# A two-layer hybrid trunk in fp32: the odd layer off GpSimd, norm squares summed by TensorE, the recurrence in halves, GELU as one function

## The chip, the cores and the metric

The kernel runs on one core of a Trainium2 chip. The metric is device time in microseconds of the whole program. One core has five engines that the text names as the profile does: PE (TensorE, matrix products into PSUM banks), DVE (VectorE), ACT (ScalarE), POOL (GpSimd) and SP (which issues DMAs).

## The reference

Two layers over a sequence of 512 positions with 1024 features, batch 1, all in fp32. Every sub-layer stands between two RMS norms, and its result is added to the residual:

```
for layer in range(2):
    hn  = rms_norm(x, norm_mix_pre[layer])
    mix = even_mixer(hn, ...) if layer == 0 else odd_mixer(hn, ...)
    x   = x + rms_norm(mix, norm_mix_post[layer])
    hn  = rms_norm(x, norm_ffn_pre[layer])
    ff  = (silu(hn @ w_gate) * (hn @ w_up)) @ w_down          # 2816 hidden
    x   = x + rms_norm(ff, norm_ffn_post[layer])
```

The even mixer is dilated attention beside an S5 state-space layer. The odd mixer, which the change touches most, is a gated recurrence:

```
z  = hn @ w_in                                   # 1024 + 1024 columns
xc = conv4(z[:, :1024]) + conv_b                 # causal, per feature
r, i = sigmoid(xc @ w_r + b_r), sigmoid(xc @ w_i + b_i)   # 4 blocks of 256
a  = exp(-8 * r * softplus(-lam))
h  = scan: h_t = a_t * h_{t-1} + sqrt(1 - a_t^2) * i_t * xc_t
mix = (h * gelu(z[:, 1024:])) @ w_out            # gelu in its tanh form
```

## The kernel before

Features lie on the 128 partitions and positions along the free dimension: the residual is eight tiles `xT[f]` of 128x512. For fp32 precision each operand of a product is split into a high and a low part in a rounded 32-bit type, and a product is three TensorE products (`mm3`: high by high, high by low, low by high). Weights are loaded raw by SP's queue (`Raw`), split by ACT (`whi`, L240) and an engine that the caller names (`wlo`, L241; VectorE unless `eng` says otherwise).

A program scheduler orders each engine's instructions by a simulated timeline. The code ties it down in three ways: `seq_of` and `pe.pin` keep an instruction behind the one traced before it on its engine, `tc.issue_after(ins)` queues what a block traces behind `ins`, and small generators (`start`, `tick`, `drain`) interleave the norm's steps with products by a counted clock.

The stages around the change, in order of time:

- **`out_proj`** (three times: `mo0` at the end of the even mixer, `fd0` after the first FFN, `mo1` after the odd mixer). It forms eight tiles of the result, four at a time. The last `ntail` contraction steps of the second four are done in two halves of 256 positions, and the post-norm of a half (`norm_half`) runs under products: column sums on TensorE, a power on GpSimd (`rstd_of`, L381), a broadcast by TensorE, and then for each feature tile a VectorE product (L492), the residual add (GpSimd, L498, but for the first), a ScalarE copy `xh` (L499) and a VectorE difference `xl` (L487). `half_cols` then multiplies these with the first four column groups of the next stage, half by half. PSUM has six `main` banks, handed out in turn, and two `side` banks.
- **`pre_rstd`** (three times: `f0`, `m1`, `f1`): the pre-norm of the next stage. ACT squares the eight `xT` tiles, VectorE adds four of them (L425), GpSimd the other four (L425), TensorE sums over partitions (`cs`), and `rstd_of` and `bcast_sb` make the row `rb`. In the FFN this is called by `mid()` after the products of the first pair of the main loop; until then the first four column groups wait as plain copies (L614, L616).
- **`ffn_up`**: 20 pairs of gate and up columns by a seven-product scheme (`f00b` to `f03b` and `f10b` to `f13b` are its banks; each pair is 84 TensorE products of 256 columns). Its weights need VectorE sums (L629 to L632) besides the splits, and its first pair needs input combinations (`tr`, `th`, `tl`, L641 on). "Head" below is this stage's first three pairs.
- **`odd_body`**: eight columns `xb`, each evacuated by `conv` (VectorE and ACT); `gates(blk)` for four blocks (sigmoids on ACT, `xc*gi` on GpSimd, L1542); `recurrence()` over all eight tiles at once (exp and tanh on ACT, the square of `a` on GpSimd, L1556, then sqrt, product, scan); `gate_product(f)` for the eight gate columns; `gate_out` (GELU from its parts: a GpSimd square L1576, VectorE, ACT's tanh, VectorE); `gated` (product with the scan, split into `y1h`, `y1l` for the output projection).

Of the kernel before, what the change touches and what calls it, by code (L numbers as in the profile page):

```python
# [11 lines left out]
F32 = mybir.dt.float32  # L12
# [3 lines left out]
ALU = mybir.AluOpType  # L16
# [3 lines left out]
P = 128  # L20
# [74 lines left out]
def hybrid_trunk(  # L95
# [318 lines left out]
    def pre_rstd(nm, keep=None):  # L414
        accs = []
        for f in (0, 4, 1, 5, 2, 6, 3, 7):
            eng = dve if f < NF // 2 else pool
            if f % (NF // 2) == 0:
                accs.append(sb.tile([P, S], F32, tag="sqacc", bufs=2, name=f"sqacc_{nm}{f}"))
                act.activation(accs[-1], xT[f], AF.Square)  # L420
            else:
                q = sb.tile([P, S], F32, tag="sq", bufs=2, name=f"sq_{nm}{f}")
                act.activation(q, xT[f], AF.Square)
                acc = accs[f // (NF // 2)]
                eng.tensor_tensor(acc, acc, q, op=ALU.add)  # L425
        return rstd_of(col_sums(lambda t: [a[:, t * P:(t + 1) * P] for a in accs], 0, NT, nm, "mid"), NT, nm,
                       keep=keep)

    def out_proj(wget, ks, yh, yl, pname, layer, nm, otile, gname, glayer, ntail, tail_alloc, early, eng0=None,
# [15 lines left out]
        for i in range(4):  # L445
# [26 lines left out]
        ready.clear()  # L472

        def norm_half(h):
# [15 lines left out]
            for f in range(NF):  # L490
# [8 lines left out]
                seq_of(act.activation(xh[f][:, HS[h]], xf, AF.Copy, scale=col(gname, glayer * NF + f)))  # L499
# [28 lines left out]
        return xh, xl, (first, bs)  # L528
# [56 lines left out]
    def ffn_up(layer, xh, xl, first, nm, hp):  # L585
# [11 lines left out]
        def mid():  # L597
            env["rb"] = bcast_sb(pre_rstd(nm, eps), nm, "mid")
# [80 lines left out]
        for n in range(NFIRST // 2, NH):  # L679
# [61 lines left out]
    def ffn(layer, xh, xl, first):  # L741
# [922 lines left out]
```

## Time and profile before

| | us |
|---|---|
| median of 3 runs (lowest to highest) | 1211.34 (1208.27 to 1212.36) |
| the profiled execution | 1211.84 |
| its span, first to last instruction | 1210.1 |

The page of the profile gives busy time by engine, the span in 40 slices of 30.25 us, the chain that ended last, and groups of instructions by line. A window's row holds, for a stretch of the span, its length, then for each engine its busy time and number of instructions, then the granted TensorE clock (1.00 is full), the DMA share and GB/s. In a waits row `A <- B: t, n, m`, A waited for B t us in all, n times, at most m. In a timeline row the numbers are start and duration; in brackets stands the idle time before it and what ended it. A line that says `x4` is four instructions merged. Matmul records are those of single passes: one fp32 product by `ones` or `ident` leaves two.

### The profile page before, as it was taken

To read this page: it belongs to the slowest core of one execution; us is meant where nothing else is said; L and a number is where in the kernel's file an instruction comes from. 1 tells how busy PE (TensorE), PEld (TensorE's weight loads), DVE (VectorE), ACT (ScalarE), POOL (GpSimd) and SP (SyncE) were. 2 spreads that over 40 slices of the span, in tenths; PEclk is the share of its full clock that TensorE was granted. 3 is DMA by queue.
4 is the path that set the end of the run, shared out by engine and by line. 5 is a ranking of instruction groups with operands and counts; after the bars stand their busy time and mean duration, and the time that the engine had idled before them with its cause. 6 is when DMAs were issued, how large, how long until landed. Compare 5 with 4: busy or idle time off the path is not lost.

```text
span 1210.1 us, 19987 instructions
## 1 busy us (share of the span) xinstructions
PE 1138.7 (94%) x7406; PEld 1012.8 (84%) x7406; DVE 905.5 (75%) x1823; ACT 622.9 (51%) x1255; POOL 181.9 (15%) x173
## 2 busy tenths in 40 slices
PE   7899999999699999999999999599799999999997
PEld 6787766888699999988889878389689999988886
DVE  7978775369789998983327897977989998894224
ACT  6555576448455545652334467354755455482222
POOL 2000020432400000000135045434310000000001
PEclk9899899999799999999999999799999999999999
DMA  8344410712233323332331223140243233343321
GB/s 207 103 137 128 110 47 1 192 36 70 70 96 105 89 79 105 107 108 94 120 96 36 87 88 105 53 135 6 69 122 97 84 100 89 105 131 105 97 69 70
DMA packets 165273, 113.44 MB, mean 94 GB/s; under 512 B 26820, under 2 KB 141752, under 8 KB 165176
## 3 DMA queue, kind: packets, MB, share of 16 engines
q1 hardware_dynamic: 161848, 109.94, 30.9%
q10 hardware_dynamic: 3040, 2.17, 0.7%
q8 instruction: 58, 0.95, 0.3%
q14 instruction: 39, 0.32, 0.1%
q0 software_dynamic: 288, 0.07, 0.0%
HBM read 103.75 MB, written 4.19 MB: 89 GB/s over the span
## 4 chain that ended last, share of the span: by engine, by line
PE 57%; DVE 6%; issue 5%; ACT 3%; DMA 3%; POOL 2%; SPq 0%; DVEq 0%; POOLq 0%; ACTq 0%
PE op_fd L170 10%; PE fo L170 10%; PE f00b L170 4%; PE f01b L170 4%; PE f02b L170 4%; PE f12b L170 4%; PE f10b L170 4%; PE f11b L170 4%; PE op_mo L170 2%; PE f03b L170 2%; PE f13b L170 2%; PE fd0b L170 2%; POOL sqacc_f L425 2%; PE xbb L170 2%; PE mo1b L170 1%
## 5 line engine op out<-in xcount | busy, mean ns | idle before, releaser
L241 DVE TENSOR_TENSOR wlo_fo<-wraw_fo,whi_fo 128x512 fp32r<-128x512 f32 x44 | 30.3, 691 | 64.0 <-PE fo L170 58.1
L170 PE MATMUL op_fd<-hi_f,whi_fd 128*128 128x512 f32 (+1 forms) x200 | 73.5, 368 | 0.0
L170 PE MATMUL op_fd<-lo_f,whi_fd 128*128 128x512 f32 (+1 forms) x200 | 73.2, 366 | 0.0
L170 PE MATMUL op_fd<-hi_f,wlo_fd 128*128 128x512 f32 (+1 forms) x200 | 72.9, 368 | 0.0
L241 DVE TENSOR_TENSOR wlo_fd<-wraw_fd,whi_fd 128x512 fp32r<-128x512 f32 x44 | 30.6, 705 | 55.2 <-ACT whi_fd L240 41.1
L170 PE MATMUL fo<-wlo_fo,hi_f 128*128 128x512 f32 x176 | 69.6, 396 | 0.0
L170 PE MATMUL fo<-whi_fo,lo_f 128*128 128x512 f32 x176 | 69.2, 394 | 0.0
L170 PE MATMUL fo<-whi_fo,hi_f 128*128 128x512 f32 x176 | 68.8, 395 | 0.0
L240 ACT ACTIVATE whi_fo<-wraw_fo 128x512 fp32r<-128x512 f32 x44 | 27.3, 631 | 71.4 <-DMA wraw_fo<-in_ffn_w_down_dram 45.1
L240 ACT ACTIVATE whi_fd<-wraw_fd 128x512 fp32r<-128x512 f32 x44 | 27.3, 630 | 56.4 <-DMA wraw_fd<-in_ffn_w_down_dram 36.4
L811 POOL TENSOR_SCALAR s<-ss,eps_f 128x1 f32<-128x1 f32 x4 | 1.1, 266 | 298.6 <-ACT fsq L809 298.6
L170 PE MATMUL op_mo<-y1l,whi_mo 128*128 128x256 f32 (+1 forms) x88 | 31.6, 361 | 13.2 <-DVE y1l L1587 13.2
L170 PE MATMUL qkv<-whi_qkv,xh_m 128*128 128x512 f32 x96 | 42.4, 443 | 1.3 <-DVE up L1196 1.0
L170 PEld LDWEIGHTS op_fd<-lo_f,whi_fd 128*128 128x128 f32 x200 | 37.7, 189 | 6.8
L170 PEld LDWEIGHTS op_fd<-hi_f,wlo_fd 128*128 128x128 f32 x200 | 37.7, 188 | 6.6
L170 PEld LDWEIGHTS op_fd<-hi_f,whi_fd 128*128 128x128 f32 x200 | 37.7, 188 | 6.4
L170 PE MATMUL qkv<-wlo_qkv,xh_m 128*128 128x512 f32 x96 | 39.3, 410 | 2.8 <-DVE wlo_qkv L241 2.8
L241 POOL TENSOR_TENSOR wlo_mo<-wraw_mo,whi_mo 128x512 fp32r<-128x512 f32 x22 | 34.0, 1576 | 50.1 <-ACT whi_mo L240 50.1
L453 POOL TENSOR_TENSOR oacc_fd<-oacc_fd,osq_fd 128x512 f32<-128x512 f32 x3 | 4.2, 1409 | 247.7 <-ACT osq_fd L452 247.6
L629 DVE TENSOR_TENSOR wraw_s_f<-wraw_f,wraw_f 128x512 f32<-128x512 f32 x40 | 27.5, 688 | 18.3 <-DMA wraw_f<-in_ffn_w_up_dram 14.1
L170 PEld LDWEIGHTS fo<-whi_fo,lo_f 128*128 128x128 f32 x176 | 33.1, 188 | 7.8
L170 PEld LDWEIGHTS fo<-whi_fo,hi_f 128*128 128x128 f32 x176 | 33.1, 188 | 7.8
(1987 smaller groups left out, 4482.7 us busy)
## 6 DMA issues: line engine op xcount, KB each, us to landing
wraw_f<-in_ffn_w_gate_dram SPq DMA_DIRECT2D x88, 256.0 KB, 3.2
wraw_f<-in_ffn_w_up_dram SPq DMA_DIRECT2D x88, 256.0 KB, 3.2
wraw_fd<-in_ffn_w_down_dram SPq DMA_DIRECT2D x44, 256.0 KB, 2.6
wraw_fo<-in_ffn_w_down_dram SPq DMA_DIRECT2D x44, 256.0 KB, 2.9
wraw_qkv<-in_ev_w_in_dram SPq DMA_DIRECT2D x24, 256.0 KB, 3.4
wraw_mo<-in_ev_w_out_dram SPq DMA_DIRECT2D x16, 256.0 KB, 4.9
wraw_xb<-in_od_w_in_dram SPq DMA_DIRECT2D x16, 256.0 KB, 3.2
wraw_gg<-in_od_w_in_dram SPq DMA_DIRECT2D x16, 256.0 KB, 3.0
```

The source lines that it names most:

```text
L170: self.pin(nc.tensor.matmul(o, lhsT=lhsT, rhs=rhs, start=start, stop=stop, **kw))
L240: act.activation(hi, src, AF.Copy)
L241: eng.tensor_tensor(lo, src, hi.bitcast(F32), op=ALU.subtract)
L425: eng.tensor_tensor(acc, acc, q, op=ALU.add)
L453: pool.tensor_tensor(acc, acc, q, op=ALU.add)
L629: dve.tensor_tensor(s1, a21, a22, op=ALU.add)
L811: pool.tensor_scalar(s0, ss[:, 0:1], 1.0 / D, eps[:, t:t + 1], op0=ALU.mult, op1=ALU.add)
```

## The change

1. `pre_rstd` goes. `norm_half` squares each half tile of the new residual on ACT right behind `xh`, and `next_sums` sums a pair of tiles over partitions by TensorE products with a column of ones into a bank `nsum` that is taken out of the six `main` banks until the stage ends. `mid()` takes `rstd_of(nsum)`.
2. In the FFN `mid()` moves ahead of the main loop; the first four column groups are evacuated with `rb` and gated at once.
3. The squares' adds in `out_proj` (L453), the `wlo` splits of `mo0`, `mo1` and the first four `xb` columns, and `xc*gi` go from GpSimd to VectorE; the square of `a` goes from GpSimd to ACT.
4. `recurrence` runs over tiles 0 to 3 after blocks 0 and 1, and over 4 to 7 after blocks 2 and 3. The sigmoids of blocks 2 and 3 are queued behind the first half's last sqrt. `gi` lies in the convolution's `xp` buffers.
5. GELU is one ACT function, queued behind the second half's last sqrt.

```diff
-    def pre_rstd(nm, keep=None):
-        ...
@@ out_proj
-                pool.tensor_tensor(acc, acc, q, op=ALU.add)
+                dve.tensor_tensor(acc, acc, q, op=ALU.add)
...
+        nb = sets["main"].pop(0)
+        share(next=(nb,))
+        nsum = bank(f"ns_{nm}", "next")
+        def next_sums(h, fs, q):
+            for i, f in enumerate(fs):
+                for t in range(2):
+                    c = 2 * h + t
+                    pe.pin(nc.tensor.matmul(nsum[:, c:c + 1], lhsT=q[:, i * HT + t * P:i * HT + (t + 1) * P],
+                                            rhs=ones[:, 0:1], start=(c == 0 and f == 0), stop=(f == NF - 1),
+                                            skip_group_check=True))
@@ norm_half, for f in range(NF)
                 seq_of(act.activation(xh[f][:, HS[h]], xf, AF.Copy, scale=col(gname, glayer * NF + f)))
+                if f % 2 == 0:
+                    q = sb.tile([P, S], F32, tag="sqacc" if h else "sq", bufs=2, name=f"nsq_{nm}{h}{f}")
+                seq_of(act.activation(q[:, HS[f % 2]], xf, AF.Square))
                 late.append(f)
+                if f % 2 and f > 1:
+                    next_sums(h, (f - 3, f - 2), qlast)
+                if f % 2:
+                    qlast = q
...
+            next_sums(h, (NF - 2, NF - 1), qlast)
@@ ffn_up
-                dve.tensor_copy(env[n][0], b)
+                dve.tensor_tensor(env[n][0], b, env["rb"], op=ALU.mult)
             else:
                 act.activation(env[n][1], b, AF.Copy)
+                gated(*env[n], n)
         heads = gemm_cols(cols2[:NFIRST], first, xh, xl, nm, evac)
         next(heads)
+        mid()
...
-            if n == NFIRST // 2:
-                mid()
-                for i in range(n):
-                    dve.tensor_tensor(env[i][0], env[i][0], env["rb"], op=ALU.mult)
-                    gated(*env[i], i)
@@ out_proj and first_cols of mo0, mo1, xb: the argument pool goes
@@ odd_body, gates
-                        t = sb.tile([P, S], F32, tag="ut", bufs=2, name=f"gi{f}")
-                    last["sig"] = act.activation(t, b, AF.Sigmoid, bias=col(bn, f)).ins
-                pool.tensor_tensor(xc[f], xc[f], t, op=ALU.mult)
+                        t = lp.tile([P, S + 3], F32, tag="xp", bufs=2, name=f"gi{f}")[:, 0:S]
+                    with ExitStack() as order:
+                        if after is not None:
+                            order.enter_context(tc.issue_after(after))
+                        last["sig"] = act.activation(t, b, AF.Sigmoid, bias=col(bn, f)).ins
+                dve.tensor_tensor(xc[f], xc[f], t, op=ALU.mult)
@@ recurrence(fs): over fs instead of all, and
-                    pool.tensor_tensor(m, al[f], al[f], op=ALU.mult)
+                    act.activation(m, a, AF.Square)
@@ gate_out goes; gate_product(f) ends with g = bank * rb
@@ gated
+            with tc.issue_after(last["sqrt"]):
+                act.activation(g, g, AF.Gelu_apprx_tanh)
             dve.tensor_tensor(g, g, xc[f], op=ALU.mult)
...
@@ the order
         gates(0)
         gates(1)
-        bs = [gate_product(0)]
-        gates(2)
-        bs.append(gate_product(1))
-        gates(3)
-        gg = [gate_out(f, bs[f]) for f in range(2)]
-        recurrence()
+        gg = [gate_product(0)]
+        recurrence(range(NF // 2))
+        gg += [gate_product(1), gate_product(2)]
+        gates(2, last["sqrt"])
+        gates(3, last["sqrt"])
+        gg.append(gate_product(3))
+        recurrence(range(NF // 2, NF))
         for f in range(NF):
-            if f >= 2:
-                bs.append(gate_product(f))
-                gg.append(gate_out(f, bs[f]))
-            if f >= 3:
-                gated(f - 3, gg[f - 3])
-        for f in range(NF - 3, NF):
             gated(f, gg[f])
+            if f + 4 < NF:
+                gg.append(gate_product(f + 4))
```

More of the change, by code (lines that the diff above doesn't have):

```diff
@@ L412, in xg_tiles @@
                 [sb.tile([P, S], F32R, tag="xl", bufs=NF, name=f"xl_{nm}{f}") for f in range(NF)])
-    def pre_rstd(nm, keep=None):
[L415 to L427, printed above, removed]
     def out_proj(wget, ks, yh, yl, pname, layer, nm, otile, gname, glayer, ntail, tail_alloc, early, eng0=None,
@@ L527, in out_proj @@
         in_order[0] = False
-        return xh, xl, (first, bs)
+        sets["main"].insert(0, nb)
+        return xh, xl, (first, bs), nsum
     def rows_of(w):
@@ L583, in ffn_cols, with ffn_up @@
         return [(w[layer], n * P) for n in range(NH) for w in (ffn_w_gate, ffn_w_up)]
-    def ffn_up(layer, xh, xl, first, nm, hp):
+    def ffn_up(layer, xh, xl, first, nsum, nm, hp):
         cols2 = ffn_cols(layer)
@@ L597, in mid @@
         def mid():
-            env["rb"] = bcast_sb(pre_rstd(nm, eps), nm, "mid")
+            env["rb"] = bcast_sb(rstd_of(nsum[:, 0:NT], NT, nm, keep=eps), nm, "mid")
         def gated(gt, ut, n):
@@ L739, in spare, with ffn @@
         return sb.tile([P, S], F32, tag="gt" if i < 2 else "ut", bufs=2, name=name)
-    def ffn(layer, xh, xl, first):
+    def ffn(layer, xh, xl, first, nsum):
         with tc.tile_pool(name=f"hid{layer}", bufs=1) as hp:
@@ L744, in ffn @@
             share(side=(6, 7))
-            hh, hl, eps = ffn_up(layer, xh, xl, first, f"f{layer}", hp)
+            hh, hl, eps = ffn_up(layer, xh, xl, first, nsum, f"f{layer}", hp)
             def otile(i, name):
@@ L757, in ffn, with ffn_last @@
             got = out_proj(rows_of(ffn_w_down[layer]), list(range(NH)), hh, hl, "p1", layer, f"fd{layer}", otile,
-                           "g0", layer + 1, 6, alloc, lambda: first_cols(odd_cols(), "xb", pool), eps=eps)
+                           "g0", layer + 1, 6, alloc, lambda: first_cols(odd_cols(), "xb"), eps=eps)
             places[:] = [p for p in places if p[0] is sb]
         return got
-    def ffn_last(xh, xl, first):
+    def ffn_last(xh, xl, first, nsum):
         hp = ctx.enter_context(tc.tile_pool(name="hid1", bufs=1))
@@ L765, in ffn_last @@
         share(side=(6, 7))
-        hh, hl, eps = ffn_up(1, xh, xl, first, "f1", hp)
+        hh, hl, eps = ffn_up(1, xh, xl, first, nsum, "f1", hp)
         xk = [None] * (2 * NT)
@@ L1522, in odd_body, with gates @@
         last = {}
-        def gates(blk):
+        def gates(blk, after=None):
             raw = Raw(4, 256, f"rg{blk}")
@@ L1550, in recurrence @@
                     last["exp"] = act.activation(gr[f], gr[f], AF.Tanh, scale=sp8[:, f:f + 1]).ins
+                    m = sb.tile([P, S], F32, tag="sq", bufs=2, name=f"lm{f}")
+                    act.activation(m, a, AF.Square)
+                    dve.scalar_tensor_tensor(gr[f], m, 1.0, gr[f], op0=ALU.add, op1=ALU.mult)
                     al.append(a)
             with tc.issue_after(last["exp"]):
-                for f in range(NF):
-                    m = sb.tile([P, S], F32, tag="sq", bufs=2, name=f"lm{f}")
-                    pool.tensor_tensor(m, al[f], al[f], op=ALU.mult)
-                    dve.scalar_tensor_tensor(gr[f], m, 1.0, gr[f], op0=ALU.add, op1=ALU.mult)
+                for f in fs:
                     last["sqrt"] = act.activation(gr[f], gr[f], AF.Sqrt).ins
-            for f in range(NF):
+            for f in fs:
                 dve.tensor_tensor(gr[f], gr[f], xc[f], op=ALU.mult)
@@ L1585, in gated @@
             l = lp.tile([P, S], F32R, tag="cl", bufs=NF, name=f"y1l{f}")
-            act.activation(h, g, AF.Copy, scale=0.5)
-            dve.scalar_tensor_tensor(l, g, 0.5, h.bitcast(F32), op0=ALU.mult, op1=ALU.subtract)
+            act.activation(h, g, AF.Copy)
+            dve.tensor_tensor(l, g, h.bitcast(F32), op=ALU.subtract)
             yh.append(h)
@@ L1628, in hybrid_trunk @@
         return
-    xh, xl, first = odd_layer(xh, xl, first)
+    xh, xl, first, nsum = odd_layer(xh, xl, first, nsum)
     for f in range(NF):
         dump(f"x3_{f}", xT[f])
-    ffn_last(xh, xl, first)
+    ffn_last(xh, xl, first, nsum)
 _INS = ['x', 'positions', 'norm_mix_pre', 'norm_mix_post', 'norm_ffn_pre', 'norm_ffn_post',
```

27 lines of the change are left out of this document (10 added, 17 removed).

## The prediction

> **What bounds the kernel now.** I read the page's busy times and slices first, then the windows, then the waits of the two places where TensorE falls back, then the timelines there.
>
> ```profile
> span 1210.1 us, 19987 instructions
> PE 1138.7 (94%) x7406; PEld 1012.8 (84%) x7406; DVE 905.5 (75%) x1823; ACT 622.9 (51%) x1255; POOL 181.9 (15%) x173
> PE   7899999999699999999999999599799999999997
> POOL 2000020432400000000135045434310000000001
> PEclk9899899999799999999999999799999999999999
> ```
>
> TensorE is the bound: 94% busy. Its dips lie where GpSimd works: slices 11, 26 and 29 (around 300, 770 and 870 us), with the granted clock down in them too. The windows show the lag. Columns: length, then busy time and count of PE, PEld, DVE, ACT, POOL, then the clock.
>
> ```profile
> 360.00:380.00 20.00, 20.00 (x170) 20.00 (x170) 20.00 (x41) 10.81 (x22) 0.00 (x0) 1.00 0.37 107
> 560.00:580.00 20.00, 20.00 (x87) 16.12 (x87) 7.03 (x11) 5.64 (x10) 0.27 (x1) 1.00 0.29 93
> 284.00:346.00 62.00, 48.20 (x330) 46.07 (x330) 50.66 (x100) 37.40 (x73) 13.89 (x5) 0.86 0.31 90
> 852.00:905.00 53.00, 41.67 (x289) 39.04 (x288) 45.34 (x90) 32.63 (x67) 13.41 (x4) 0.90 0.30 86
> 667.00:760.00 93.00, 92.09 (x406) 74.28 (x404) 80.16 (x126) 57.56 (x94) 34.40 (x25) 1.00 0.30 91
> 760.00:807.00 47.00, 32.38 (x115) 24.48 (x114) 45.85 (x55) 21.33 (x36) 17.74 (x12) 0.82 0.29 90
> ```
>
> The first two rows are TensorE undisturbed: 20/170 = 0.118 us for a product of 256 columns, 20/87 = 0.230 us for one of 512. By these prices the 330 products of the first FFN head (284 to 346) need 38.8 us and took 62: 23.2 lost. The second head (852 to 905): 289 need 34.0 of 53: 19.0 lost. Odd output projection (760 to 807): 115 need 26.4 of 47: 20.6 lost. Until 760 the odd layer loses nothing. Together 62.8 us, lost clock included. What ends the waits:
>
> ```profile
> PE f02b L170 <- ACT pv_f L696: 4.6, 1, 4.6
> ACT sq_f L423 <- POOL sqacc_f L425: 7.8, 1, 7.8
> PE f12b L170 <- ACT pv_f L696: 5.6, 1, 5.6
> PE op_mo L170 <- DVE y1l L1587: 13.2, 2, 9.8
> ```
>
> In the heads TensorE waits for a ScalarE copy, and ScalarE stands behind a square whose buffer GpSimd holds. The timeline says why GpSimd holds it so long:
>
> ```profile
> 302.76 9.46 POOL L425 TENSOR_TENSOR sqacc_f<-sqacc_f,sq_f 128x512 f32<-128x512 f32 x1 [18.72 <-issue]
> 303.06 0.68 DVE L629 TENSOR_TENSOR wraw_s_f<-wraw_f,wraw_f 128x512 f32<-128x512 f32 x1
> ...
> 310.42 0.68 DVE L241 TENSOR_TENSOR wlo_f04c<-wraw_s_f,whi_f04c 128x512 fp32r<-128x512 f32 x1
> 660.21 1.30 POOL L425 TENSOR_TENSOR sqacc_m<-sqacc_m,sq_m 128x512 f32<-128x512 f32 x1
> 312.25 0.63 ACT L423 ACTIVATE sq_f<-xT 128x512 f32<-128x512 f32 x1 [7.85 <-POOL sqacc_f L425]
> ```
>
> The same add takes 1.30 us elsewhere. Here it ends 1.1 us after VectorE's unbroken run does: it was shut out for 8.2 us. In the odd layer it goes the other way round:
>
> ```profile
> 712.69 6.63 POOL L1542 TENSOR_TENSOR xc<-xc,gi 128x512 f32<-128x512 f32 x4 [2.05 <-ACT gi L1541]
> 712.38 0.68 DVE L241 TENSOR_TENSOR wlo_rg<-wraw_rg,whi_rg 128x512 fp32r<-128x512 f32 x1
> 712.98 1.78 DVE L1508 SCALAR_TENSOR_TENSOR xc<-xp,cols,xc 128x512 f32<-128x512 f32 x1
> ```
>
> While GpSimd runs, a VectorE instruction of 0.68 takes 1.78 us: 1.10 extra. The last two windows count 25 and 12 GpSimd instructions, by the code 34 of them whole tiles (8 `xc*gi`, 8 squares of `a`, 8 of GELU's, 10 `wlo_mo`). That is up to 37 us lost on an engine that is 45.85 of 47 us busy and that TensorE waits for.
>
> The Trainium skill, SBUF — State Buffer, section "Who interferes with whom", says that a VectorE instruction with two SBUF inputs and a GpSimd instruction that reads SBUF exclude each other, for one whole instruction. The 1.78 us agree; the 9.46 us, over a dozen VectorE instructions, go beyond it.
>
> **The change, part by part.**
>
> *Odd layer without GpSimd.* VectorE gains 8 products `xc*gi` and 10 `wlo_mo` (18 at 0.68 us: 12.2), loses two instructions of each of 8 GELUs (16: 10.9), and loses the 37 us of collisions. Net some 36 us less, against 13.2 of waiting: the 20.6 us go, if nothing else is late. The other 12 `wlo_mo`, 8 `wlo_xb` and 9 squares' adds that come to VectorE (29 at 0.68: 20 us in all) fall in output projections such as 560 to 580, where it is 7.03 of 20 us busy: nothing, and at most 20 us if that cover were gone.
>
> *Squares on TensorE.* Per output projection 32 one-column products, three times 32 in all, replace three times 8. Their price:
>
> ```profile
> 668.40 1.62 PE L170 MATMUL cs_m<-ones,sqacc_m 128*128 128x1 f32 x14
> L170 PE MATMUL cs_m<-ones,sqacc_m x16: 165/250/250, 666.5 to 669.8; 128*128 128x1 f32 x16
> L170 PEld LDWEIGHTS cs_f<-ones,sqacc_f x32: 186/192/338, 323.2 to 888.0; 128*128 128x128 f32 x32
> ```
>
> Eight products leave 16 records, and 14 records take 1.62 us: 0.116 a record, 0.23 a product. If weight loads (0.19 a record) did not overlap it were 0.38. I take 0.23, the pace actually seen: 96 cost 22.3 us, 24 that go save 5.6; the upper end adds 14. They stand in tails where TensorE has no gap, so all of it counts. ScalarE's 48 half squares replace 24 whole ones:
>
> ```profile
> 266.00 0.40 ACT L518 ACTIVATE oqs_mo<-o_mo 128x256 f32<-128x256 f32 x1
> 275.74 0.48 DVE L492 SCALAR_TENSOR_TENSOR o_mo<-o_mo,cols,bc_mo 128x256 f32<-128x256 f32 x1 [1.33 <-PE bc_mo L170]
> 284.07 0.51 ACT L499 ACTIVATE xh_mo<-xT,cols 128x256 fp32r<-128x256 f32 x1 [0.37 <-POOL xT L498]
> ```
>
> In the tail ScalarE idles 0.37 us before each copy, waiting for GpSimd's residual add, and a square of 0.40 at most fits there: nothing, or 8 times 0.03 a half. One bank fewer in the tail makes its second block wait for one ScalarE copy, covered by the first.
>
> *FFN heads.* With the adds gone the 23.2 and 19.0 us go, except what GpSimd did not cause: waits for the splits of weights and inputs, and for `gt_f`. In the first head:
>
> ```profile
> PE f00b L170 <- DVE gt_f L711: 2.1, 1, 2.1
> PE f01b L170 <- ACT whi_f03b L240: 1.4, 1, 1.4
> PE f03b L170 <- ACT th_f L658: 1.1, 1, 1.1
> PE f00b L170 <- ACT whi_f03a L240: 0.9, 1, 0.9
> ```
>
> These are 5.5 us. The heads' products now start 7.4 us (32 times 0.23) later, behind a preparation that starts as before and so is further ahead; I keep half, 3 us a head, the second taken like the first, and add 1 us a head for the broadcast `rb`, which the evacuation now needs at once: 8 us. The ends are 0 and 13 us. Behind that evacuation on VectorE's queue stand the splits of the next pair of weights, and behind its four banks the products of the second pair; if `rb` is late, both wait, which is the first rival.
>
> The two SiLUs with their table load come forward into the same stretch, 1.28 and twice 0.63 us at most (ScalarE rows below and above) on an engine 37.40 of 62 us busy, which loses eight squares there: nothing.
>
> *Recurrence in halves.* No arithmetic more except 8 squares on ScalarE (57.56 of 93 us busy), but order: the sigmoids of blocks 2 and 3 stand behind the first half's square roots, and three more table loads come (sigmoid, exponential, root again; GELU takes the place of tanh).
>
> ```profile
> 728.47 1.28 ACT L1549 ACT_TABLE_LOAD   x1
> 729.77 5.02 ACT L1549 ACTIVATE ga<-gr,nsp 128x512 f32<-128x512 f32 x8
> 677.49 1.29 DVE L1504 TENSOR_TENSOR xp<-fd0b,bcs_m 128x512 f32<-128x512 f32 x2 [1.03 <-ACT bcs_m L405]
> 696.58 0.68 ACT L1541 ACTIVATE gi<-rg,cols 128x512 f32<-128x512 f32 x1
> 720.40 0.68 DVE L1512 TENSOR_TENSOR cl<-xc,ch 128x512 fp32r<-128x512 f32 x1
> ```
>
> A load costs 1.28 us, and the next activation starts 0.02 after it: 3.9 us. GELU as one function is not in the trace; I take tanh's kind of price, and its bounds are 0.63 (ACT's 128x512 instructions) and one load more. The moved block loads (two DMAs a block on SP's queue, now behind two gate weights) keep their number. One wait is new and not in the change's words: `gi` now lies in the convolution's `xp` buffers, two of them, so the first two `gi` sigmoids, at 696.58 now, must wait for the convolutions of features 6 and 7, whose end is 720.40. Eight convolutions of five VectorE instructions of 0.68 are 27 us; begun at 677.49 as now and without collisions they end near 705. TensorE can go on meanwhile until its six banks are full (36 products of 0.230: 8 us). I take 4 us, between 0 and 16 (an end at 721 less 696.58 less 8). With 3.9 for the loads the odd layer keeps 8 us of waits.
>
> The Trainium skill, ScalarE: Activation LUTs, section "Table sets: the hidden batching unit", speaks against the halves: all exponentials first, then all roots. Its section "What ACT_TABLE_LOAD costs" prices a switch at 2.66 us with a drain, by which three would be 8.0 and the sum 4.1 longer; the load's 1.28 us agree, the 0.02 us behind it show no drain.
>
> **Sum.** -62.8 - 5.6 + 22.3 + 8 + 8 = -30.1 us. The profiled execution took 1211.84 us (span 1210.1), 0.5 over the median 1211.34: 1181.7, said as 1181.
>
> **The rivals.** *GpSimd's power is shut out instead* (15%). The change leaves GpSimd the small power for `rb`, now asked for inside VectorE's unbroken run of the head. If each waits 8.2 us as the add did, TensorE stands at the broadcast: +16.4, 1198. Against it:
>
> ```profile
> 892.38 1.01 POOL L381 TENSOR_TENSOR rsy_f<-rst_f,neghalf 128x4 f32<-128x4 f32 x1 [7.34 <-DVE rst_f L378]
> ```
>
> That ran unhindered between VectorE instructions. By the Trainium skill's rule above the power could wait for one instruction at most, and this rival would cost next to nothing.
>
> *The odd layer turns from VectorE to ScalarE* (13%): the `gi` wait at its end of 16 us, 12 above what I took, and 4 more (three loads again) where sigmoids queue behind the first half's roots and TensorE runs out of banks: 1197. For it: ScalarE's stage is in order and its roots wait for VectorE. Against it: 28 us of gate products (120 of 0.230) lie between the last block and the projection.
>
> *The sums hold up TensorE* (10%, slower). If the order puts the one-column products ahead of the products that would cover them, TensorE waits for the last square of each half: from 275.74 to 285.0 (the last copy, 284.07 and 0.51, and a square) are 9.2 us, of which 2.8 are three of the half's four groups of sums: 6.4 for each of six halves, 38 us: 1219. It decides from 5.0 us a half. For it: they are pinned in program order. Against it: only to the product traced before, so later ones may pass.
>
> *Both the first two* (5%): 1213, no change.
>
> **How the numbers follow.** The forecast has 57%; its own range is 1166 (no waits stay) to 1195 (weight loads bare). Low 1166, high 1206 leaves out the last two rivals and little more. Faster by over 0.3% (3.6 us, about what this kernel's spread can tell): 57 + 15 + 13 = 85%; same 5%; slower 10%.
>
> **What would show it.** Right: no GpSimd 128x512 instruction after 220 us; VectorE's maxima in the odd layer below 0.8 us except scans; heads' first three pairs within 35 us; one-column products 0.23 us each, 7.4 us a tail; seven table loads in the odd layer. Wrong: TensorE waiting for `rsy`, for `gi`, or for the new squares, or VectorE still full around 770 us with none of GpSimd beside it.

## The result, and the profile after

The changed kernel takes 1177.17 us (median; 1172.18 to 1182.99) against 1211.01 of the kernel before, timed beside it: a ratio of 0.9725, with a 95% interval of 0.9676 to 0.9775. The forecast was 1181, from 1166 to 1206. The profiled execution of the changed kernel, at 1172.18 us, is the shortest of its times; the one of before, 1211.84, lies in their middle. So the two traces differ by 39.7 us and the medians by 33.8. One of six executions of mixed_sums (experiment 11), at 1257.35 us with a granted clock of 0.839, was slow and is left out of its median.

The page of the changed kernel, its span, two lines of busy times and three of slices:

```profile
span 1170.2 us, 20253 instructions
PE 1129.9 (97%) x7550; PEld 1010.3 (86%) x7550; DVE 878.1 (75%) x1841; ACT 629.2 (54%) x1290; POOL 60.5 (5%) x101
PE   6899999999999999999999999999999999999997
POOL 2000010004000000000002200004000000000001
PEclk9899999999999999999999999999999999999999
```

All three dips of TensorE are gone, and so are the dips of the granted clock under them. GpSimd's 182 us have become 60. The heads start at other times now, so the windows are laid from the first FFN product of each head over 35 us. The other two have the times that they had before; the odd output projection now begins at 749.9 us instead of 761.4, so the third row holds its start and the fourth its rest and what follows. Columns: length, then busy time and count of PE, PEld, DVE, ACT, POOL, then the clock.

```profile
297.00:332.00 35.00, 32.73 (x268) 31.92 (x267) 34.69 (x69) 23.44 (x48) 0.00 (x0) 1.00 0.38 107
831.00:866.00 35.00, 32.48 (x262) 31.31 (x261) 33.43 (x68) 23.88 (x49) 0.00 (x0) 1.00 0.38 107
667.00:760.00 93.00, 92.92 (x400) 74.77 (x399) 78.91 (x128) 73.70 (x120) 0.00 (x0) 1.00 0.33 99
760.00:807.00 47.00, 45.87 (x310) 41.91 (x308) 28.64 (x58) 21.00 (x44) 7.30 (x9) 1.00 0.29 86
```

The heads run with VectorE and TensorE almost equally full (34.69 and 32.73 of 35 us), and the odd layer with TensorE full to 0.08 us. The waits for `y1h` and `y1l` ahead of the projection, 14.4 us before, are not in the view any more. What is left of TensorE's waits at the changed places is small:

```profile
PE op_mo L170 <- ACT oacc_mo L434: 2.4, 1, 2.4
PE f01b L170 <- ACT pu_f L703: 2.1, 2, 1.2
PE f11b L170 <- DVE tl_f L668: 1.2, 1, 1.2
PE ns_mo L468 <- ACT nsq_mo L500: 1.1, 4, 0.4
PE ns_fd L468 <- ACT nsq_fd L500: 0.8, 3, 0.3
```

The first was 0.3 us before. TensorE waits for a bank that ScalarE's square frees, and that square stands behind splits of FFN weights that have to wait for their load:

```profile
242.31 0.63 ACT L240 ACTIVATE whi_f<-wraw_f 128x512 fp32r<-128x512 f32 x1 [1.36 <-DMA wraw_f<-in_ffn_w_up_dram]
243.66 0.58 ACT L434 ACTIVATE oacc_mo<-op_mo 128x512 f32<-128x512 f32 x1
```

The last two of the waits above are those for the new squares. The one-column products, one GELU group and two groups of VectorE in the odd layer (busy, mean ns):

```profile
273.74 0.95 PE L468 MATMUL ns_mo<-ones,nsq_mo 128*128 128x1 f32 x8
740.53 2.20 ACT L1583 ACTIVATE gg<-gg 128x512 f32<-128x512 f32 x4
L1512 DVE SCALAR_TENSOR_TENSOR xc<-xp,cols,xc 128x512 f32<-128x512 f32 x20 | 14.2, 744 | 0.0
L1569 DVE TENSOR_TENSOR_SCAN xc<-ga,gr 128x512 f32<-128x512 f32 x8 | 9.7, 1217 | 0.0
```

Eight records, four products, take 0.95 us: 0.12 a record, as forecast. GELU as one function costs 0.55 us a tile, and of VectorE's groups in the odd layer none but the scans has a mean above 0.75 us.

**Where the time came from.** A span can be split in three: TensorE's waiting (span less its busy time), the part of its busy time that is lost to the clock (busy time times one less the granted clock, summed over windows of half a microsecond), and the rest, the work at full clock. A low clock while TensorE waits costs nothing more than the wait, so it is not counted twice. The mean clock of the two kernels, from the view of the cores:

```profile
core 0: 1210.1 us, clock 0.973
core 0: 1170.2 us, clock 0.995
```

Over the whole spans that is 32.7 and 5.9 us, of which 8.0 and 1.2 lie in waits. Before: 71.4 waiting, 24.7 clock, 1114.0 work. After: 40.3, 4.7, 1125.2. So 31.1 us came from waits, 20.0 from the clock, and 11.2 went to more work, the one-column products. The profiled execution of the change was lucky in its clock: the other three have 0.982, 0.993 and 0.988, a loss of 21.3, 8.2 and 14.1 us over the span. That is most of what sets the change's 1172 from its 1183 us, and most of the 5.9 us between the difference of the traces and that of the medians. The clock goes down in stretches, each behind a wait. Before, in the first head, around the odd projection, and in the second head:

```profile
311.00:319.00 8.00, 4.76 (x24) 4.76 (x25) 4.75 (x10) 4.97 (x11) 1.21 (x1) 0.57 0.09 25
328.00:336.00 8.00, 7.80 (x40) 7.80 (x41) 5.07 (x11) 2.44 (x5) 1.16 (x2) 0.57 0.14 42
765.00:776.00 11.00, 4.00 (x10) 3.14 (x10) 11.00 (x13) 5.26 (x8) 3.48 (x2) 0.53 0.30 95
874.00:882.00 8.00, 6.18 (x30) 6.19 (x31) 6.92 (x11) 6.38 (x14) 1.79 (x1) 0.57 0.28 81
```

Eight us at 0.57 are 3.4 us of lost clock, eleven at 0.53 are 5.2; of these, TensorE waited through a part (from 765 to 776 it was busy for 4.00 us). In steps of one microsecond, every stretch found in any of these traces loses about 1.7, 3.4, 5.1 or 6.8 us, but for the one that the program's end breaks off: half the clock for one, two, three or four spells of 3.4 us. The Trainium skill, TensorE: Matmul & The Clock Gate, section "What's actually happening", has this: half rate after an idle window of about 3.4 us, in windows that run freely. The length and the half agree with the rows; what sets it off does not quite (below).

### The profile page after: what moved, and what is told of

It is laid out like the page before. It is cut to its first block, busy times and chain, and to the rows that moved or that the text cites. A ratio compares the mean times of both kernels' runs of the same rounds, so it can differ in the third digit from the quotient of the medians.

```text
span 1170.2 us, 20253 instructions
## 1 busy us (share of the span) xinstructions
PE 1129.9 (97%) x7550; PEld 1010.3 (86%) x7550; DVE 878.1 (75%) x1841; ACT 629.2 (54%) x1290; POOL 60.5 (5%) x101
## 4 chain that ended last, share of the span: by engine, by line
PE 78%; ACT 8%; DMA 6%; DVE 5%; issue 2%; POOL 1%; SPq 0%; ACTq 0%; DVEq 0%; POOLq 0%
PE fo L170 10%; PE op_fd L170 10%; PE qkv L170 5%; PE f00b L170 5%; PE f02b L170 5%; PE f01b L170 4%; PE f11b L170 4%; PE op_mo L170 4%; PE f12b L170 4%; PE f10b L170 4%; PE gg L170 3%; PE f03b L170 2%; PE f13b L170 2%; PE xbb L170 2%; PE fd0b L170 2%
## 5 line engine op out<-in xcount | busy, mean ns | idle before, releaser
L240 ACT ACTIVATE whi_fo<-wraw_fo 128x512 fp32r<-128x512 f32 x44 | 27.6, 631 | 70.2 <-DMA wraw_fo<-in_ffn_w_down_dram 43.8
L170 PEld LDWEIGHTS fo<-wlo_fo,hi_f 128*128 128x128 f32 x176 | 33.1, 188 | 7.5
L170 PE MATMUL qkv<-whi_qkv,xl_m 128*128 128x512 f32 x96 | 39.0, 407 | 0.0
L638 DVE TENSOR_TENSOR wraw_s_f<-wraw_f,wraw_f 128x512 f32<-128x512 f32 x40 | 27.3, 683 | 10.6 <-DMA wraw_f<-in_ffn_w_up_dram 7.5
L241 DVE TENSOR_TENSOR wlo_mo<-wraw_mo,whi_mo 128x512 fp32r<-128x512 f32 x32 | 21.4, 685 | 15.3 <-ACT whi_mo L240 15.1
L639 DVE TENSOR_TENSOR wraw_t_f<-wraw_s_f,wraw_f 128x512 f32<-128x512 f32 x40 | 27.2, 681 | 5.6 <-DMA wraw_f<-in_ffn_w_gate_dram 5.6
```

Of the source, the lines that this page charges most:

```text
L170: self.pin(nc.tensor.matmul(o, lhsT=lhsT, rhs=rhs, start=start, stop=stop, **kw))
L240: act.activation(hi, src, AF.Copy)
L241: eng.tensor_tensor(lo, src, hi.bitcast(F32), op=ALU.subtract)
L638: dve.tensor_tensor(s1, a21, a22, op=ALU.add)
L639: dve.tensor_tensor(s2, s1, a11, op=ALU.subtract)
```

## The experiments

The same split for all kernels, each from its profiled execution. The last column has the lost clock over the whole span (span times one less the mean granted clock), of the trace and as the median of the kernel's executions; for the kernel before, of the 59 that were timed beside the experiments. It tells how far a trace is like the others of its kernel. Medians of the time were taken beside the kernel before, which had 1208.7 to 1211.0.

| kernel | median us | span | waiting | clock | work | whole span's clock: trace, median |
|---|---|---|---|---|---|---|
| before | 1211.01 | 1210.1 | 71.4 | 24.7 | 1114.0 | 32.7, 32.6 |
| the change | 1177.17 | 1170.2 | 40.3 | 4.7 | 1125.2 | 5.9, 11.2 |
| adds_vector | 1203.83 | 1203.3 | 71.2 | 19.3 | 1112.8 | 26.5, 32.5 |
| odd_alone | 1199.31 | 1203.5 | 66.0 | 27.8 | 1109.7 | 31.3, 28.7 |
| sums_alone | 1195.42 | 1193.1 | 54.2 | 11.4 | 1127.5 | 16.7, 17.9 |
| odd_adds_vector | 1188.72 | 1186.2 | 57.3 | 20.2 | 1108.7 | 22.5, 23.7 |
| pair_sums | 1202.95 | 1200.3 | 67.8 | 22.4 | 1110.1 | 30.0, 30.6 |
| sums_twice | 1204.73 | 1202.7 | 28.3 | 35.5 | 1138.9 | 37.3, 33.0 |
| whole_recurrence | 1187.11 | 1182.9 | 48.3 | 9.5 | 1125.1 | 14.2, 16.6 |
| gelu_parts | 1178.38 | 1176.1 | 41.6 | 9.5 | 1125.0 | 10.6, 12.4 |
| odd_gpsimd | 1180.83 | 1182.1 | 41.8 | 16.0 | 1124.3 | 17.7, 13.0 |
| idle_mults | 1190.21 | 1187.1 | 49.9 | 10.8 | 1126.4 | 14.2, 16.0 |
| mixed_sums | 1195.74 | 1195.6 | 53.9 | 25.0 | 1116.7 | 29.9, 25.0 |
| late_sums | 1190.67 | 1188.6 | 54.4 | 18.1 | 1116.1 | 20.2, 20.2 |

The work column follows the number of one-column products almost alone: 1109 to 1114 with 24 of them (the old column sums, and pair_sums), 1116 to 1117 with 48, 1124 to 1128 with the change's 96, 1139 with 192. All else that moved the time is waiting and clock. Where a text below sets clock against the change, some 5 us of the difference are the luck of the change's trace.

**1. The starved add taken out of the kernel before (adds_vector).**

```diff
 def pre_rstd(nm, keep=None):
-            eng = dve if f < NF // 2 else pool
+            eng = dve
```

> The kernel before, with one edit: the four adds of squares that GpSimd made in each pre-norm go to VectorE; order, TensorE sums and odd layer stay as they were. Theory (the heads lost their time to a GpSimd add shut out by VectorE's unbroken run): the heads win back most of 42.2 us, less 8 to 11 us of waits that GpSimd did not cause, so 1177 to 1183. Rival (the heads are cured by taking the squares out of them and making rb early; VectorE, 19.7 of 20 us busy there, cannot take three more adds): 1192 or more.

Measured: 1203.83, ratio 0.9957 (0.9942 to 0.9972): 5 us. The rival was nearer. The view of waits of the first head (284 to 346), and its window:

```profile
PE cs_f L170 <- DVE sqacc_f L425: 2.9, 2, 2.6
PE f01b L170 <- DVE pu_f L712: 2.8, 1, 2.8
PE f00b L170 <- DVE gt_f L711: 2.0, 1, 2.0
284.00:346.00 62.00, 50.20 (x354) 48.12 (x353) 53.71 (x108) 39.56 (x77) 1.01 (x1) 0.89 0.33 94
```

No wait for GpSimd is left, and the window still loses the clock (0.89) and 12 us of TensorE. The squares' adds are now 0.68 us each on VectorE, which has no gap from 286 to 318 us; TensorE waits for VectorE's evacuation, for the sums, and for the late `rb` (`gt_f`). So the starved add was a wait in front of a full VectorE, not the whole loss.

**2. The odd layer's half of the change alone (odd_alone).** The squares and `rb` stay as before.

```diff
# the change, but
-            env["rb"] = bcast_sb(rstd_of(nsum[:, 0:NT], NT, nm, keep=eps), nm, "mid")
+            env["rb"] = bcast_sb(pre_rstd(nm, eps), nm, "mid")
# and without next_sums and the half squares of the tails
```

> The change without its sums: odd layer, weight splits and output projections free of GpSimd, recurrence in halves, GELU as one function; pre-norm squares, their GpSimd adds and the order of the FFN heads as before. Theory: the odd layer's 20.6 us come back and nothing else, 1189 to 1193, and the GpSimd add of 9 us stands in both heads again. Rival (the one-column sums are the change's gain): within 5 us of before.

Measured: 1199.31, ratio 0.9924 (0.9902 to 0.9946): some 9 us, half of what was expected. Its trace, at 1205.41 us, is the slowest of its nine executions. The gain at the projection is there, but a new wait stands ahead of it, in the view of waits from 660 to 800, and GpSimd's add is starved in the head as before (timeline):

```profile
PE rg L170 <- ACT gr L1547: 6.7, 2, 6.4
308.74 9.68 POOL L425 TENSOR_TENSOR sqacc_f<-sqacc_f,sq_f 128x512 f32<-128x512 f32 x1 [18.50 <-ACT sq_f L423]
```

TensorE runs out of banks because the sigmoids of the second half's gates stand behind the first half's roots. That is the prediction's second rival. It bites here and not in the change because `rb` comes later behind the last product of `xb`, and the convolutions, the sigmoids and the roots follow it. The kernels with halves bear this out: where the last product of the broadcast starts 0.9 us behind, the wait for `rg` is 0 to 0.9 us, with 3.7 (late_sums) it is 2.7, with 4.4 (mixed_sums) 1.9, with 5.4 (pair_sums) 3.1, with 8.5 (odd_adds_vector) 4.9, and here, with 10.2, it is 6.7.

**3. TensorE's sums alone (sums_alone).** The odd layer and GpSimd's other work stay as before.

```diff
# before, with the change's out_proj, ffn_up and rb
-            env["rb"] = bcast_sb(pre_rstd(nm, eps), nm, "mid")
+            env["rb"] = bcast_sb(rstd_of(nsum[:, 0:NT], NT, nm, keep=eps), nm, "mid")
```

> The kernel before with only the sums changed: squares in the tail, one-column sums on TensorE, rb ahead of the FFN's main loop; odd layer and GpSimd's splits as before. Theory: heads win 42.2 less 8, TensorE pays 22.3 less 5.6: 1191 to 1196. Rival (sums hide in gaps of TensorE): 1180 or less.

Measured: 1195.42, ratio 0.9905 (0.9877 to 0.9932), as expected. The split against before is 17.2 less waiting, 13.3 less clock, 13.5 more work. The heads are cured by this part alone; the projection still waits 13.3 us for `y1l`.

**4. The change with the old squares, all adds on VectorE (odd_adds_vector).** As experiment 2, with experiment 1's edit.

```diff
# odd_alone, and
-            eng = dve if f < NF // 2 else pool
+            eng = dve
```

> The change, but the pre-norm squares and their order as before with all adds on VectorE, none on TensorE or GpSimd. Theory: both gains without the price of the sums, 1211 less 20.6 less 30 = 1158 to 1165, below the change. Rival (TensorE sums are needed to free VectorE in the heads): 1177 or more.

Measured: 1188.72, ratio 0.9846 (0.9822 to 0.9869). The rival was right: without GpSimd, but with the squares summed in the head, 11.5 us are missing against the change. The work is 16.5 us less than the change's, and 17.0 of waiting and 15.5 of clock take its place; the largest waits are 4.9 us for `rg`, and 4.2 and 3.2 for VectorE's `pu_f` in the two heads.

**5. VectorE adds, TensorE sums a quarter (pair_sums).**

```diff
-                if f % 2 and f > 1:
-                    next_sums(h, (f - 3, f - 2), qlast)
                 if f % 2:
-                    qlast = q
+                    if f == 1:
+                        qacc = q
+                    else:
+                        seq_of(dve.tensor_tensor(qacc, qacc, q, op=ALU.add))
... (the squares' buffers change too)
-            next_sums(h, (NF - 2, NF - 1), qlast)
+            next_sums(h, (0, NF - 1), qacc)
```

> The change, but VectorE adds the four square tiles of a half (3 adds a half, 0.68 us each), so that TensorE sums 8 instead of 32 one-column products in each tail. Theory of the prediction (every one-column product lengthens the time, none stands in a gap): 72 products of 0.23 us fewer, 16.6 us: 1160 to 1165. Rival (the FFN heads are set by VectorE, which the trace after shows 61.39 of 62 us busy there; the products of the first two tails stand in time that TensorE would lose in the heads anyway, so only the third tail's 24 count, 5.5 us, and VectorE's 4 us of adds a tail take some of it back): 1171 to 1180.

Measured: 1202.95, ratio 0.9946 (0.9927 to 0.9966), worse than both theories. The work fell by 15.1 us (72 products at 0.23 are 16.6); waiting rose by 27.5 and the clock's loss by 17.7. Its waits and two of its windows:

```profile
PE ns_mo L468 <- DVE nsq_mo L506: 8.6, 3, 5.7
PE ns_fd L468 <- DVE nsq_fd L506: 7.1, 2, 5.6
639.00:653.00 14.00, 8.35 (x41) 8.11 (x41) 4.53 (x11) 2.40 (x6) 2.37 (x3) 0.51 0.00 0
823.00:834.00 11.00, 6.63 (x33) 6.63 (x33) 2.97 (x8) 1.63 (x4) 2.37 (x3) 0.53 0.00 0
```

This is the wait of the prediction's slower rival, with VectorE's adds in the place of ScalarE's squares: the sums, pinned in order, hold TensorE until VectorE's last add. The half clock does not come from these waits alone. It begins at 639.2 us, 0.2 before the wait of 5.6, when TensorE had waited 1.2 us for a column sum at 636; in the second window it begins at 823.5, 1.8 us into the wait.

**6. Each sum twice (sums_twice).**

```diff
+                    pe.pin(nc.tensor.matmul(nsum[:, 8 + c:9 + c], lhsT=q[:, i * HT + t * P:i * HT + (t + 1) * P],
+                                            rhs=ones[:, 0:1], start=False, stop=(f == NF - 1),
+                                            skip_group_check=True))
```

> The change, with each one-column product issued twice, the second into columns that nobody reads. Theory of the prediction (a product costs its 0.23 us wherever it stands): 96 more, 22 us: 1197 to 1202. Rival (they delay TensorE's start on a head behind a VectorE that is still preparing; each head still lost 3.8 and 4.5 us, and so much of each tail's added 7.4 us is taken back): 14 us, 1188 to 1194.

Measured: 1204.73, ratio 0.9969 (0.9945 to 0.9993): 27.6 us more than the change, over both theories. Waiting is the least of all kernels, 12.0 below the change against 13.7 more work, and the two heads have one wait of 0.9 us left: the later start on the heads does give back waits, as the rival had it, and nearly all that the products cost. But the clock takes 30.8. Two windows over the 32 records that now stand in a row, and two rows of the timeline in them:

```profile
292.00:294.00 2.00, 2.00 (x21) 2.00 (x19) 1.61 (x4) 2.00 (x5) 0.53 (x1) 1.00 0.11 28
294.00:296.00 2.00, 2.00 (x12) 2.00 (x13) 2.00 (x4) 2.00 (x5) 0.00 (x0) 0.56 0.38 111
293.84 0.36 PE L468 MATMUL ns_mo<-ones,nsq_mo 128*128 128x1 f32 x2
295.18 0.56 PE L468 MATMUL ns_mo<-ones,nsq_mo 128*128 128x1 f32 x2
```

TensorE waits for nothing here, and the clock is halved all the same, from the middle of the run of one-column products on; the products of 256 columns behind them pay. The clock falls so at each of the kernel's six half tails, three times in or behind a run of 32 records (3.8 to 5.3 us) and three times behind runs of 15 or 16 close together, and TensorE has no wait above 0.6 us there. In the change the longest runs are eight records, 0.95 us, and the clock stays.

**7. One recurrence over all features (whole_recurrence).**

```diff
         gg = [gate_product(0)]
-        recurrence(range(NF // 2))
-        gg += [gate_product(1), gate_product(2)]
-        gates(2, last["sqrt"])
-        gates(3, last["sqrt"])
-        gg.append(gate_product(3))
-        recurrence(range(NF // 2, NF))
+        gates(2)
+        gg.append(gate_product(1))
+        gates(3)
+        gg += [gate_product(2), gate_product(3)]
+        recurrence(range(NF))
```

> The change, with the recurrence of all eight features behind the gates of all blocks, as before, and two table loads of the odd layer fewer or more by the order that results. Theory (what freed the odd output projection is that GpSimd is gone; the halves matter little): 1175 to 1182. Rival (the halves are what feeds the projection in time): the projection waits for the last output tiles, 8 us or more: 1186 or over.

Measured: 1187.11, ratio 0.9823 (0.9801 to 0.9846): 9.9 us more than the change, the rival's answer. The odd projection waits again although no GpSimd instruction runs near it:

```profile
PE op_mo L170 <- ACT y1h L1587: 4.7, 1, 4.7
PE op_mo L170 <- DVE y1l L1588: 4.0, 1, 4.0
744.00:768.00 24.00, 15.30 (x53) 11.44 (x52) 23.47 (x35) 13.37 (x22) 0.00 (x0) 0.79 0.14 46
```

8.7 us of waits and a window at 0.79 (24 times 0.21: 5.0 us of clock, 3.1 of them while TensorE was busy). VectorE is full, 23.47 of 24.

**8. GELU from its parts, without GpSimd (gelu_parts).** Square and tanh on ScalarE, two more instructions on VectorE for each tile.

```diff
-            with tc.issue_after(last["sqrt"]):
-                act.activation(g, g, AF.Gelu_apprx_tanh)
+            act.activation(t, g, AF.Square)
+            dve.scalar_tensor_tensor(t, t, 1.0 / GELU_B, g, op0=ALU.add, op1=ALU.mult)
+            act.activation(t, t, AF.Tanh, scale=GELU_A * GELU_B)
+            dve.scalar_tensor_tensor(g, t, 1.0, g, op0=ALU.add, op1=ALU.mult)
... (and the factor 0.5 in the copies to y1h, y1l)
```

> The change, with GELU from its parts (a square and a tanh on ScalarE, two more instructions of VectorE for each of eight tiles, none on GpSimd). Theory (VectorE without GpSimd has 11 us to spare under 28 us of gate products): 1176 to 1181. Rival (the single function is what freed VectorE in time for the output projection): 8 us or more: 1185 or over.

Measured: 1178.38, ratio 0.9742 (0.9724 to 0.976), as expected: the single function is worth nothing that can be told from no change.

**9. The odd layer's tile work back on GpSimd (odd_gpsimd).**

```diff
-                dve.tensor_tensor(xc[f], xc[f], t, op=ALU.mult)
+                pool.tensor_tensor(xc[f], xc[f], t, op=ALU.mult)
-                    act.activation(m, a, AF.Square)
+                    pool.tensor_tensor(m, a, a, op=ALU.mult)
-                        alloc, lambda: first_cols(ffn_cols(1), "f1"))
+                        alloc, lambda: first_cols(ffn_cols(1), "f1"), pool)
```

> The change, with the odd layer's tile work back on GpSimd: the eight products by the input gate, the eight squares of the decay, and the low halves of the output projection's early weights; halves and single-function GELU stay. Theory A (the collisions between GpSimd and VectorE were what made the projection late): TensorE waits for the projection's operands again and the granted clock falls after it: 1189 or over. Theory B (it was the order, all gates before one recurrence; with halves VectorE's stretched instructions lie under the gate products): 1175 to 1183.

Measured: 1180.83, ratio 0.9769 (0.9745 to 0.9793); its interval overlaps the change's. Theory B: the collisions are back, but hidden. They are 26 of the 34 whole tiles, as GELU's eight squares stay away. One of VectorE's groups, and the odd layer's window:

```profile
L1569 DVE TENSOR_TENSOR_SCAN xc<-ga,gr 128x512 f32<-128x512 f32 x8 | 11.8, 1480 | 0.0
667.00:760.00 93.00, 92.77 (x398) 74.28 (x397) 86.55 (x113) 67.58 (x107) 29.65 (x21) 1.00 0.28 85
```

VectorE's instructions are stretched (1480 ns against 1217 for a scan) and GpSimd is busy 29.65 us, and TensorE still loses only 0.23 of 93 us.

**10. GpSimd work in the heads that nobody reads (idle_mults).**

```diff
         next(heads)
         mid()
+        for f in range(8):
+            z = sb.tile([P, S], F32, tag="sqacc", bufs=2, name=f"idle_{nm}{f}")
+            pool.tensor_tensor(z, xT[f], env["rb"], op=ALU.mult)
```

> The change, plus eight GpSimd products of whole tiles in the head of each FFN (a tile of the residual by the broadcast factor), which nobody reads. Theory A (a GpSimd instruction is shut out by VectorE's unbroken run, takes several us, and hurts only who waits for it): the products take 3 us or more each on the whole, the time stays at 1174 to 1183. Theory B (GpSimd stretches VectorE, which is 61.39 of 62 us busy in the head): VectorE instructions of 0.68 us take 1.8, eight of them a head, and TensorE waits for what stands behind: 1188 or over.

Measured: 1190.21, ratio 0.9856 (0.9833 to 0.988): 13.0 us more than the change. Theory B. Timelines of GpSimd and VectorE in the first head:

```profile
300.43 12.48 POOL L631 TENSOR_TENSOR idle_f<-xT,bcs_f 128x512 f32<-128x512 f32 x8 [8.31 <-ACT bcs_f L405]
300.85 1.77 DVE L241 TENSOR_TENSOR wlo_f03a<-wraw_f,whi_f03a 128x512 fp32r<-128x512 f32 x1
302.54 1.78 DVE L642 TENSOR_TENSOR wraw_t_f<-wraw_s_f,wraw_f 128x512 f32<-128x512 f32 x1
```

The eight products are not shut out: 1.56 us each. VectorE is what suffers, 1.77 for 0.68, until they are done. So GpSimd in a head costs on both sides: the first add of a head was starved (before), and a run of products stretches VectorE.

The starving is not the rule for a single add either. The next one of the same head, in the kernel before, met VectorE in a run without a gap and took a turn:

```profile
878.56 1.79 POOL L425 TENSOR_TENSOR sqacc_f<-sqacc_f,sq_f 128x512 f32<-128x512 f32 x1 [4.77 <-ACT sq_f L423]
879.13 1.77 DVE L241 TENSOR_TENSOR wlo_f14a<-wraw_f,whi_f14a 128x512 fp32r<-128x512 f32 x1
```

**11. Half of the sums on VectorE (mixed_sums).**

```diff
+                    if f == 1:
+                        qacc = q
+                    elif f < NF - 1:
+                        seq_of(dve.tensor_tensor(qacc, qacc, q, op=ALU.add))
+                    else:
+                        next_sums(h, (0, 1), qacc)
+                        qlast = q
... (the squares' buffers change too)
```

> The change, but VectorE adds the first three square tiles of each half (two adds of 0.68 us), summed by TensorE one tile later, so that nothing waits at the end as it did when VectorE added all four; the last tile is summed as now. 48 products of 0.23 us fewer, 11.0 us. Theory A (each product costs its time, as the prediction has it): 1164 to 1169. Theory B (in front of a head whose VectorE is full, TensorE's 3.7 us are given back as waits there, and a wait can cost a stretch at half clock of 1.7 or 3.4 us more): 1173 to 1186.

Measured: 1195.74, ratio 0.989 (0.9871 to 0.9909), worse than theory B. The work is 8.5 us less (48 products at 0.23 are 11.0); 13.6 of waiting and 20.3 of clock came in their place. The tail of the FFN, its waits and the window behind them:

```profile
PE ns_fd L468 <- DVE nsq_fd L506: 2.5, 1, 2.5
PE cs_fd L170 <- ACT oqs_fd L528: 1.2, 1, 1.2
641.00:652.00 11.00, 8.54 (x40) 8.54 (x41) 3.57 (x9) 3.25 (x8) 3.32 (x4) 0.53 0.00 0
```

Two waits of 1.2 and 2.5 us, within 5 us of each other, cost 3.7 us, and 4.3 more of clock while TensorE was busy. The clock falls at 641.7 us, 0.75 into the second wait: in the 3.4 us ahead of that TensorE had waited 1.95.

**12. The same, with the first half's sums issued later (late_sums).**

```diff
# mixed_sums, but the first half's sums only in the second half
+                        if h:
+                            next_sums(0, (0, 1), held[0])
+                            next_sums(0, (NF - 2, NF - 1), held[1])
...
```

> As the last experiment (VectorE adds three of a half's four square tiles, 48 products fewer), but the first half's sums are issued two tiles into the second half, where they are ready, so that TensorE doesn't stand before them; the second half's come at the end, as in the change. Theory A (each product costs its 0.23 us, and the last experiment lost its 11 us only by the wait before its sums and the half clock behind it): 1164 to 1172. Theory B (TensorE's products cover time in which it would wait in the tails and heads anyway, VectorE's adds lengthen that time, and each wait brings a stretch at half clock): 1176 to 1200.

Measured: 1190.67, ratio 0.9847 (0.9822 to 0.9872). Theory B. The wait before the sums is gone, 5.1 us came back, and 13.5 are still missing against the change with 9.1 us less work. In the tails TensorE waits 1.2 to 1.9 us at places where the change has a run of sums to issue, and the clock falls behind it. And the sums end late, behind VectorE's adds: `rb` is broadcast at 303.5 to 304.6, after the head's first ten products, where the change has it done at 298.1, ahead of the first. Two windows, just before the first evacuation and in the third pair:

```profile
297.00:302.00 5.00, 5.00 (x45) 5.00 (x44) 2.93 (x10) 2.59 (x5) 1.33 (x1) 1.00 0.57 163
332.00:337.00 5.00, 3.37 (x26) 3.17 (x26) 5.00 (x12) 2.19 (x4) 0.00 (x0) 1.00 0.32 96
```

VectorE is idle for two of five us while `rb` is awaited and full ever after, and TensorE waits for it: three pairs take 41.7 us (302.30 to 343.97), 8 more than in the change, 1.7 of them a stretch of half clock.

## Why the prediction was right, and where it was not

The total was forecast at 1181 and measured at 1177; against the traces the forecast change was -30.1 and the measured one -39.7. That the median lies nearer to the forecast than the trace is chance: a median execution of the change loses 5.3 us more to the clock than the profiled one.

- *The 62.8 us lost in three places.* Right, and all but what was kept for the heads went. The prediction knew that lost clock was in them but not how much: 62 times 0.14, 53 times 0.10 and 47 times 0.18, from its own windows, are 22.4 us, of which some 17 fell on products and the rest on waits.
- *One-column products, 22.3 less 5.6 us.* The size was about right: work rose by 11.2 us against before and by 16.5 against experiment 4, which has the old sums and most of the change's rest, where 16.7 were forecast. What failed is the sentence beside it, that all of it counts because there is no gap in the tails. Experiment 6 shows it best: 96 products more are 13.7 us of work, and 12.0 of waiting go. Experiments 5, 11 and 12 put adds on VectorE in the place of products and get slower. They show that this exchange loses (in the odd layer the broadcast of `rb` then starts 3.7 to 5.4 us behind the last product of `xb`, in the change 0.9), and not that a product is free.
- *The heads' 8 us.* Right. Three pairs of 84 products need 29.7 us at 0.118; the first head took 33.7 (297.83 to 331.51) and the second 34.3 (831.04 to 865.37): 4.0 and 4.6 lost.
- *The odd layer's 8 us.* Mis-sized: it was 0.08. The prediction began the convolutions at 677.49 us, as before, and so had the first `gi` sigmoids wait until near 705. With `rb` early they began at 661.0 and ended at 696.6, and the first `gi` sigmoid ran at 695.6. The seven table loads are there, and the gate products covered them. Experiments 2 and 4 show how near it was: with `rb` 8 to 9 us later, TensorE waits up to 6.4 and 4.9 us at that place.
- *"With the adds gone the 23.2 and 19.0 us go"*, with GpSimd's starved add as the cause. Half right: the time went, but taking only GpSimd out of the adds gave 5 us (experiment 1). What cured the heads was their squares out of VectorE and ScalarE, `rb` at their start, and TensorE arriving later, three things that no experiment here takes apart: sums_alone gives 13.6 with GpSimd still at work elsewhere.
- *The odd projection's 20.6 us, laid to 37 us of collisions.* The step that failed in its cause. The collisions are real (experiment 9), but with 26 of the 34 put back TensorE has no wait ahead of the projection (1180.83 in all), and with the halves undone and GpSimd away it loses 9.9 us. The prediction had the halves as a cost; they are what feeds the projection early. Undoing each of the two alone costs 9.9 and about 3.7 us of 20.6 (the 3.7 within what the intervals allow), so either covers part of what the other does.
- *The rivals.* GpSimd's power ran in 1.06 and 1.07 us in the heads. The wait of sums on ScalarE's squares was 0.4 us a half at most, far under the 5.0 at which it decides; with VectorE in the chain (experiment 5) it was 5.6, and the kernel fell back to 1203.
- *Not foreseen:* the wait at the even layer's projection, 2.4 us where it was 0.3. It goes with the splits and adds that left GpSimd there, which were booked at nothing: the three kernels that have them on GpSimd (before, adds_vector, sums_alone) wait 0 to 0.4 us at that place, the other eleven 1.0 to 3.2. The adds themselves run only behind the wait (from 245.41 us); why ScalarE's splits meet their load later is open.

The parts do not add: odd_alone 9.7 and sums_alone 13.6 below the 1208.99 of before in their comparison make 23.3, the change 33.8. That they need each other is shown by the `rg` wait of experiments 2 and 4. That the rest is the clock is read from the split, and not shown by an experiment that changes the clock alone.

Still open: why the first GpSimd add of a head is shut out for 9 us by an unbroken run of VectorE, while later adds of the head and a row of eight products take their turn between VectorE's instructions. The first is GpSimd's first instruction for over 18 us; whether that matters no run here tests.

## What to carry to other kernels

Split a span into waiting, clock and work before pricing a change: a wait of TensorE costs itself and often one or two spells of 1.7 us behind it, and a second small wait nearby can cost more than both waits. A low clock under a wait is not a second loss. Look at the clock of every execution, too: one trace may be a lucky one. Work for the bound engine is not always a cost: put where it would wait, small products can take an operation from the engine that feeds it and start the next stage's scalars earlier. But keep such products apart: close runs of 15 to 32 one-column records were followed by half the clock here, runs of eight were not.

## What the runs showed of the hardware that was not expected

- The clock is halved by less than an idle spell of 3.4 us. The section of the Trainium skill's page TensorE: Matmul & The Clock Gate on "HAM oscillation" gives gaps over about 3.4 us as the rule. Here a wait of 1.2 us in the 3.4 us ahead was enough in experiment 5, and 1.95 us in two pieces in experiment 11. And the same wait may or may not: at the even projection mixed_sums had 1.92 us without work in the first window below and then ran at 0.60; the change had 2.41 there and kept 1.00 (the two pairs of windows, mixed_sums first). That fits windows that run freely, and it may be why the change's four executions lose 5.9 to 21.3 us to the clock and take 1172 to 1183.

```profile
241.00:245.00 4.00, 2.08 (x9) 1.32 (x8) 4.00 (x8) 2.34 (x5) 0.00 (x0) 1.00 0.45 128
245.00:249.00 4.00, 3.83 (x10) 3.08 (x11) 3.81 (x7) 2.84 (x6) 0.00 (x0) 0.60 0.00 0
...
241.00:245.00 4.00, 1.59 (x7) 0.99 (x6) 4.00 (x8) 2.50 (x5) 0.00 (x0) 1.00 0.35 103
245.00:249.00 4.00, 4.00 (x19) 3.25 (x18) 3.90 (x7) 2.86 (x6) 0.00 (x0) 1.00 0.00 0
```

- One-column products in a row of 32 records (3.8 to 5.3 us), or in rows of 15 or 16 close together, were followed by half the clock with TensorE hardly waiting (experiment 6).
- GpSimd and VectorE exclude each other in turns of one instruction when GpSimd has several in a row (1.56 and 1.77 us, experiment 10), which is what the Trainium skill, SBUF — State Buffer, section "Who interferes with whom", says; the second add of a head did so too (1.79 and 1.77 us). The first add of each head was held for 9.32 to 9.68 us (before and experiment 2), which goes beyond it.
